# Where split weights begin in memory: token-major units 32 bytes behind a multiple of 128, the others on one

## The chip, the cores and the metric

The kernel runs on one core of one Trainium2 chip. The metric is the device time of one execution in microseconds (us); the median of several runs counts. Before the change three runs took 1570.54, 1565.43 and 1568.50 us.

## The reference, cut to what matters

A decoder trunk of two layers over 256 tokens of width 1024. Each layer is a half-step SwiGLU FFN, a token-mixing sub-layer (a Mamba-2 branch and a gated DeltaNet branch on the same normalised input), and a second half-step FFN. Everything is float32.

```python
for l in range(DEPTH):                                   # DEPTH = 2
    h = h + 0.5 * swiglu(rms_norm(h, ffn1_norm[l]), ffn1_w_in[l], ffn1_w_out[l])
    u = rms_norm(h, mix_norm[l])
    (z_s, xbc, dt_s, qkv, z_d, b_d, a_d, gate_s, gate_d) = jnp.split(u @ w_in[l], split_points, axis=-1)
    y_s = mamba2_branch(z_s, xbc, dt_s, ...)
    y_d = deltanet_branch(qkv, z_d, b_d, a_d, ...)
    merged = (jax.nn.sigmoid(gate_s) * (y_s @ ssm_w_branch[l])
              + jax.nn.sigmoid(gate_d) * (y_d @ dn_w_branch[l]))
    h = h + merged @ w_out[l]
    h = h + 0.5 * swiglu(rms_norm(h, ffn2_norm[l]), ffn2_w_in[l], ffn2_w_out[l])
return rms_norm(h, final_norm)
```

The large products (`u @ w_in`, the FFN's and the projections) hold nearly all of the work.

## The kernel before, in words

**Split weights.** TensorE multiplies in a reduced float32 form (`fp32r`), so each weight is split into a high part and the rest, and a product is made of three: high by high, high by low, low by high. Weights come from memory in forms of 128 rows by 1024 values (4096 bytes in each partition), in an order laid out on the host. `load` brings a form into a raw buffer `wraw` (five of them; a few go into `wfirst`). `prep` makes the two parts of it: ScalarE writes the high part into `whi` (line 66, the helper `act`), VectorE writes the rest into `wlo` (line 69, the helper `tt`). There are five buffers of `whi` and five of `wlo`, used in turn. `take` hands out the next pair of parts and keeps loads and splits some forms ahead.

**Who multiplies with what.** A matmul has a stationary operand of 128x128, loaded by a weight load of its own (PEld in the profile) while an earlier matmul runs, and a moving operand of 256 or 512 columns that streams past it.

- Token-major units (`tok_chunk`, called for `f`, the first four forms of an FFN, and for `t`, the z and gate units of the mixer): the normalised, transposed input `uT` is stationary, the split weights are moving, 512 columns. `mm3`, lines 287 to 289.
- Products with activations made in the kernel (`out_chunks` and `block_products`, results `p`, `o`, `b`): activations `gh`, `gl`, `bsa` to `bsd`, `bh`, `bl`, `mh`, `ml` are stationary, the split weights are moving, 512 columns. Also `mm3`, lines 287 to 289.
- Channel-major units: the split weights are stationary, `uT` is moving. `chan_pair` (`fc`, lines 342 and 346: one matmul of 512 and one of 256 columns) and `chan_chunk` (`kk`, `qq`, `vv`, `xs`, `bc`, `zd`, lines 292 to 294: 256 columns).

The order of the units is written out by hand: `FFN` and `ORDER` at the top of the file, and in them the order of the matmuls on TensorE is fixed.

**Where the buffers lie.** The pools are laid one behind the other in each partition, each tile rounded up to 32 bytes. In the kernel before, by the allocation that its build makes:

| Tiles | First byte | Byte modulo 128 |
|---|---|---|
| `cs` with the identity (`cpool`) | 24704 | 0 |
| `uT` (`cpool`) | 32928 | 32 |
| `wraw`, five of 4096 bytes (`wpool`) | 57984 | 0 |
| `whi`, five of 4096 bytes (`wpool`) | 78464 | 0 |
| `wlo`, five of 4096 bytes (`wpool`) | 98944 | 0 |
| `gh`, `gl`, `bsa`, `bsb`, `bsc`, `mh`, `ml` and all other tiles of `slots` | 119424 and on | 0 |
| `bh`, `bl`, `bsd` and the other 2048-byte tiles of `s2` | 203392 and on | 0 |

The matmuls' operands begin at multiples of 128 bytes within their tiles, so these remainders are those of the operands. The last byte in use is 228128.

Of the kernel before, what the change touches and what calls it, by code (L numbers as in the profile page):

```python
# [8 lines left out]
F32R = mybir.dt.float32r  # L9
I32 = mybir.dt.int32  # L10
AF = mybir.ActivationFunctionType
ALU = mybir.AluOpType
# [4 lines left out]
P = 128  # L17
D = 1024
S = 256
DEPTH = 2  # L20
# [9 lines left out]
NRAW = 5  # L30
NSPL = 5
START = 2

FFN = "f" + 8 * "c" + "A" + 4 * "c" + "A" + 4 * "c" + "A" + 2 * "c" + "A" + 2 * "c" + "BdBBBddddd"
# [7 lines left out]
ORDER = """  # L44
# [7 lines left out]
def trunk_kernel(ctx, tc, x, wst, wsm, norms, lpar, rpar, cst, out):  # L52
    nc = tc.nc
    V, A, G, PE = nc.vector, nc.scalar, nc.gpsimd, nc.tensor

    cpool = ctx.enter_context(tc.tile_pool(name="cpool", bufs=1))
    wpool = ctx.enter_context(tc.tile_pool(name="wpool", bufs=1))
# [7 lines left out]
    def act(o, i, func=AF.Copy, **kw):  # L65
        return A.activation(out=o, in_=i, func=func, **kw)  # L66

    def tt(o, a, b, op):
        return V.tensor_tensor(out=o, in0=a, in1=b, op=op)  # L69
# [9 lines left out]
    def f(ap):  # L79
        return ap.bitcast(F32)  # L80

    def tmp2(name):
        return s2.tile([P, 512], F32, tag="s2", name=name)
# [52 lines left out]
    n_forms = len(plan)  # L136
# [3 lines left out]
    def load(j):  # L140
# [5 lines left out]
        state["last"] = nc.sync.dma_start(r[:], wst[stream[j] // 2, :, (stream[j] % 2) * 1024 :][:, 0:1024])  # L146
        raws[j] = r

    def prep(i):
        kind, js, _ = plan[i]  # L150
        hi = wpool.tile([P, 1024], F32R, tag="whi", name="whi", bufs=NSPL)
        lo = wpool.tile([P, 1024], F32R, tag="wlo", name="wlo", bufs=NSPL)

        def less(o, a, b):
            tt(raws[js[o]][:], raws[js[a]][:], raws[js[b]][:], ALU.subtract)


        r = raws[js[{"q2": 1, "q4": 4, "q5": 3}.get(kind, 0)]]
        with ExitStack() as behind:
            for ins in state["behind"].pop(i, ()):  # L160
                behind.enter_context(tc.issue_after(ins))
            act(hi[:], r[:])
            if kind == "q1":
                less(1, 2, 1)
            elif kind == "q2":
                less(0, 2, 0)
            elif kind == "q4":
                less(0, 3, 0)
            tt(lo[:], r[:], f(hi[:]), ALU.subtract)
            if kind == "q0":  # L170
                less(0, 1, 0)
        for o in {"d": (0,), "q2": (1,), "q3": (2,), "q4": (4,), "q5": (3,), "q6": (0,)}.get(kind, ()):
            raws.pop(js[o])
        halves[i] = (hi, lo)

    def ahead(key, n, fn):
        while state[key] < n:
            fn(state[key])
            state[key] += 1

    def take():
        j = state["taken"]
        state["taken"] = j + 1
        ahead("loaded", min(plan[min(j + NSPL, n_forms) - 1][2] + NRAW - 1, n_raw), load)
        ahead("prepped", min(j + 1 if state["hold"] else j + NSPL, n_forms), prep)
        return halves.pop(j)
# [46 lines left out]
    def rstd_of(t):  # L233

        ss = small([P, 2], "ss")
        for n in range(2):
            junk = tmp2("junk")
            state["square"] = act(junk[:], h[:, t, n * 512 : (n + 1) * 512], AF.Square, scale=1.0 / 32.0, accum_out=ss[:, n : n + 1])
        z = small([P, 2], "zz")
        ts(z[:, 0:1], ss[:, 0:1], ss[:, 1:2], ALU.add, EPS, ALU.add)  # L240
        rsqrt(z[:, 1:2], z[:, 0:1], [P, 1])
        return z[:, 1:2]
# [18 lines left out]
    def norm_in(nw, add=None):  # L261

        for t in range(2):
            with tc.high_priority(offset=PRI), ExitStack() as behind:
                if add:
                    add(t)
                    if t == 0:
                        behind.enter_context(tc.issue_after(state["sums"][5].ins))
                ins, done = rms_chain(t, nw)
            if t == 0:  # L270
                state["hold"] = False
                n = state["taken"]
                if not add:
                    ahead("prepped", n + 1, prep)
                    with tc.issue_after(done[0].ins), tc.issue_after(done[1].ins):
                        ahead("prepped", n + START, prep)
                with tc.issue_after(ins.ins):
                    ahead("prepped", n + 2, prep)
                if add:
                    state["behind"][n + 2] = [d.ins for d in done]  # L280
            elif add:

                state["behind"][n + 4] = (state["square"].ins, ins.ins)
                state["input"] = done
# [946 lines left out]
    for t in range(2):  # L1231
        add(t)
        o = [tmp2("fo") for _ in range(2)]
# [3 lines left out]
        r = rstd_of(t)  # L1237
# [137 lines left out]
```

## Time and profile before

| What | Value |
|---|---|
| Runs | 1570.54, 1565.43, 1568.50 us; median 1568.5 us |
| Profiled execution, first to last instruction (span) | 1565.8 us |
| TensorE (PE) busy | 1545.0 us, 99% of the span, 10152 matmuls |
| Weight loads (PEld) busy | 1342.0 us, 86% |
| VectorE (DVE) busy | 1302.4 us, 83% |
| ScalarE (ACT) busy | 999.8 us, 64% |
| Granted TensorE clock | 0.999 |

The span is the time from the first to the last instruction of the profiled execution; the profile gives no other time for it, and the span lies 2.7 us below the median of the three runs. Matmuls overlap: the duration of one runs from its start to its modelled end, and the next one starts before that end. What a matmul costs is therefore the distance from its start to the start of the next, which the timeline shows; durations can be compared only between matmuls of one shape. In a row `t<-wlo,uT` the tile written stands first, then the moving operand, then the stationary one.

### The profile page before, as it was taken

The numbers are of one execution on the slowest core, as the hardware profiler recorded it, in microseconds if no ns is written. First come the engines' busy times: TensorE is split into PE (matmuls) and PEld (weight loads), VectorE is DVE, ScalarE is ACT, GpSimd is POOL, SyncE is SP. The second block draws the span as 40 slices with busy tenths as digits, with TensorE's granted clock in tenths as the row PEclk, the third lists the DMA queues.
The fourth block names the chain that finished last, engine by engine and source line by source line (L and its number), as shares of the span: only waits on it lengthen the run. The fifth ranks groups of instructions, "written<-read, shape, count | busy, mean of one in ns | idle before, by whom it ended". The sixth has DMA issues, their size and how long they took to land.

```text
span 1565.8 us, 26672 instructions
## 1 busy us (share of the span) xinstructions
PE 1545.0 (99%) x10152; PEld 1342.0 (86%) x10152; DVE 1302.4 (83%) x2048; ACT 999.8 (64%) x1694; POOL 53.2 (3%) x60
## 2 busy tenths in 40 slices
PE   8999999999999999999999999999999999999998
PEld 6888779999888888888788887899998888888886
DVE  6889969957899766899878998699579996679897
ACT  6666668766675655666566676686656666466664
POOL 0000010000000000000000001010000000000000
PEclk9999999999999999999999999999999999999999
DMA  8565565553455555465765566555336546555553
GB/s 298 197 214 188 195 212 173 178 158 118 174 207 173 177 205 196 159 210 177 262 204 187 168 198 223 189 189 189 116 123 213 177 166 212 201 175 166 198 189 134
DMA packets 94215, 292.99 MB, mean 187 GB/s; under 512 B 22325, under 2 KB 23301, under 8 KB 93062
## 3 DMA queue, kind: packets, MB, share of 16 engines
q1 hardware_dynamic: 94086, 291.29, 55.2%
q8 instruction: 79, 1.29, 0.3%
q14 instruction: 50, 0.41, 0.1%
HBM read 289.33 MB, written 1.92 MB: 186 GB/s over the span
## 4 chain that ended last, share of the span: by engine, by line
PE 76%; DVE 13%; DMA 5%; issue 3%; ACT 2%; POOL 1%; SPq 0%; POOLq 0%; DVEq 0%; ACTq 0%
PE fc L342 15%; PE fc L346 8%; DVE wlo L69 7%; PE t L287 3%; PE t L288 3%; PE t L289 3%; DMA wraw<-in_wst_dram 3%; PE b L289 3%; PE b L288 3%; PE b L287 2%; PE xs L292 2%; PE xs L293 2%; PE xs L294 2%; PE o L288 1%; PE o L289 1%
## 5 line engine op out<-in xcount | busy, mean ns | idle before, releaser
L69 DVE TENSOR_TENSOR wlo<-wraw,whi 128x1024 fp32r<-128x1024 f32 x488 | 591.0, 1221 | 139.8 <-ACT whi L66 136.1
L66 ACT ACTIVATE whi<-wraw 128x1024 fp32r<-128x1024 f32 x488 | 511.6, 1057 | 176.4 <-PE b L289 29.8
L342 PE MATMUL fc<-uT,whi 128*128 128x512 f32 x1280 | 445.5, 391 | 0.0
L346 PE MATMUL fc<-uT,wlo 128*128 128x256 f32 x1280 | 360.9, 282 | 0.0
L342 PEld LDWEIGHTS fc<-uT,whi 128*128 128x128 f32 x1280 | 240.3, 188 | 50.7
L346 PEld LDWEIGHTS fc<-uT,wlo 128*128 128x128 f32 x1280 | 241.8, 189 | 0.8
L287 PE MATMUL t<-whi,uT 128*128 128x512 f32 x256 | 102.9, 403 | 0.0
L288 PE MATMUL t<-wlo,uT 128*128 128x512 f32 x256 | 101.5, 396 | 0.2 <-DVE wlo L69 0.2
L289 PE MATMUL t<-whi,uT 128*128 128x512 f32 x256 | 101.5, 397 | 0.0
L66 ACT ACTIVATE whi<-wfirst 128x1024 fp32r<-128x1024 f32 x64 | 67.8, 1059 | 29.7 <-DVE wfirst L69 20.4
L66 ACT ACTIVATE sg<-fc 128x256 f32<-128x256 f32 x80 | 30.6, 382 | 82.3 <-PE fc L346 82.3
L69 DVE TENSOR_TENSOR wlo<-wfirst,whi 128x1024 fp32r<-128x1024 f32 x64 | 78.1, 1220 | 2.0 <-ACT whi L66 1.9
L287 PE MATMUL b<-whi,bh 128*128 128x512 f32 x192 | 76.1, 398 | 0.0
L288 PE MATMUL b<-wlo,bh 128*128 128x512 f32 x192 | 74.9, 390 | 0.0
L289 PE MATMUL b<-whi,bl 128*128 128x512 f32 x192 | 74.3, 394 | 0.3 <-DVE bl L69 0.3
L292 PE MATMUL xs<-uT,whi 128*128 128x256 f32 x256 | 73.1, 286 | 0.0
L294 PE MATMUL xs<-uT,wlo 128*128 128x256 f32 x256 | 71.6, 280 | 0.0
L293 PE MATMUL xs<-uT,whi 128*128 128x256 f32 x256 | 71.4, 279 | 0.0
L288 PE MATMUL o<-wlo,gh 128*128 128x512 f32 x160 | 64.6, 404 | 2.6 <-DVE wlo L69 2.5
L69 DVE TENSOR_TENSOR wfirst<-wraw,wfirst 128x1024 f32<-128x1024 f32 x48 | 58.6, 1220 | 8.9 <-DMA wraw<-in_wst_dram 8.9
L289 PE MATMUL o<-whi,gl 128*128 128x512 f32 x160 | 62.5, 391 | 0.0
L287 PE MATMUL o<-whi,gh 128*128 128x512 f32 x160 | 62.1, 392 | 0.0
(317 smaller groups left out, 3424.5 us busy)
## 6 DMA issues: line engine op xcount, KB each, us to landing
wraw<-in_wst_dram SPq DMA_DIRECT2D x504, 512.0 KB, 4.5
wfirst<-in_wst_dram SPq DMA_DIRECT2D x16, 512.0 KB, 5.8
dc<-rdram SPq DMA_DIRECT2D x8, 1024.0 KB, 8.4
nw<-in_norms_dram SPq DMA_DIRECT2D x6, 512.0 KB, 6.2
gb<-rdram SPq DMA_DIRECT2D x8, 256.0 KB, 5.3
h<-in_x_dram SPq DMA_DIRECT2D x4, 256.0 KB, 5.7
out_dram<-fo SPq DMA_DIRECT2D x4, 256.0 KB, 2.1
dq<-X SPq DMA_DIRECT2D x2, 256.0 KB, 5.0
```

The lines of the kernel that those rows point to most:

```text
L66: return A.activation(out=o, in_=i, func=func, **kw)
L69: return V.tensor_tensor(out=o, in0=a, in1=b, op=op)
L287: PE.matmul(ps, lh, rh, start=start, stop=False)
L288: PE.matmul(ps, lh, rl, start=False, stop=False)
L289: return PE.matmul(ps, ll, rh, start=False, stop=stop)
L292: PE.matmul(ps, wh, mh, start=start, stop=False)
L293: PE.matmul(ps, wh, ml, start=False, stop=False)
L294: PE.matmul(ps, wl, mh, start=False, stop=stop)
L342: PE.matmul(ps[a][:], wh[:, c0 : c0 + P], uT[:, kt].rearrange("p o t -> p (o t)"), start=kt == 0, stop=False,)
L346: PE.matmul(ps[a][:, 0:S], wl[:, c0 : c0 + P], uTh[:, kt, :], start=False, stop=kt == KT - 1)
```

## The change

Each `whi` and `wlo` tile becomes 4192 bytes instead of 4096, and the kernel uses 4096 bytes of it that begin `skip` values into the tile. Because 4192 is 96 more than a multiple of 128, the five buffers of a tag begin at five different remainders; `base` works out the remainder of the buffer that form `i` gets (`turn` is the order in which the buffers are handed out), and `skip` makes up the rest to the place that `places(i)` asks for: 32 bytes behind a multiple of 128 for the forms of the token-major units (`f` and `t` in the list `uses`), a multiple of 128 for every other form. High and low part get the same place. Nothing else is edited; the instructions, their order and their shapes stay.

```diff
+BASE = (0, 96)
...
+    uses = []
+    for _ in range(DEPTH):
+        for sub in range(2):
+            for kind in FFN:
+                uses += {"f": "ffff", "c": "cc", "A": "pppp", "B": "ppp", "d": "o"}[kind]
+            if sub == 0:
+                uses += 4 * "t"
+                for name in ORDER:
+                    uses += {"z": "tt", "g": "tt", "N": 8 * "b"}.get(name[0], "hh" if name[0] in "kqvdbx" and len(name) > 1 else "")
+                uses += 16 * "b" + 8 * "w"
+    assert len(uses) == n_forms, (len(uses), n_forms)
+    turn = [0, 4, 3, 2, 1]
+
+    def places(i):
+        return (1, 1) if uses[i] in "ft" else (0, 0)
+
+    def split_tile(i, o, tag):
+        r = places(i)[o]
+        j = (turn[i % 5], turn[i % 5])[o]
+        base = (BASE[o] + 96 * j) % 128
+        skip = (32 * r - base) % 128 // 4
+        return wpool.tile([P, 1024 + 24], F32R, tag=tag, name=tag, bufs=NSPL)[:, skip : skip + 1024]
+
     def prep(i):
         kind, js, _ = plan[i]
-        hi = wpool.tile([P, 1024], F32R, tag="whi", name="whi", bufs=NSPL)
-        lo = wpool.tile([P, 1024], F32R, tag="wlo", name="wlo", bufs=NSPL)
+        hi = split_tile(i, 0, "whi")
+        lo = split_tile(i, 1, "wlo")
...
-            act(hi[:], r[:])
+            act(hi, r[:])
...
-            tt(lo[:], r[:], f(hi[:]), ALU.subtract)
+            tt(lo, r[:], f(hi), ALU.subtract)
```

## The prediction

> **What bounds the kernel now.** I read the busy times first, then the chain that ended last, the granted clock, and then the stretches in which the touched units run.
>
> ```profile
> span 1565.8 us, 26672 instructions
> PE 1545.0 (99%) x10152; PEld 1342.0 (86%) x10152; DVE 1302.4 (83%) x2048; ACT 999.8 (64%) x1694; POOL 53.2 (3%) x60
> PEclk9999999999999999999999999999999999999999
> PE 76%; DVE 13%; DMA 5%; issue 3%; ACT 2%; POOL 1%; SPq 0%; POOLq 0%; DVEq 0%; ACTq 0%
> 193.10:232.50 39.40, 38.34 (x176) 29.83 (x175) 25.30 (x44) 25.23 (x34) 7.56 (x5) 1.00 0.62 217
> 407.60:423.70 16.10, 15.07 (x75) 12.19 (x74) 13.91 (x16) 9.40 (x15) 1.01 (x1) 1.00 0.44 173
> 439.10:450.00 10.90, 10.90 (x49) 8.80 (x48) 10.30 (x15) 7.80 (x12) 1.60 (x1) 1.00 0.60 193
> 157.70:192.80 35.10, 34.58 (x153) 27.27 (x152) 31.93 (x39) 22.12 (x27) 0.55 (x1) 1.00 0.55 187
> 532.00:579.40 47.40, 47.40 (x227) 39.06 (x226) 29.47 (x39) 25.14 (x37) 0.69 (x1) 1.00 0.64 219
> ```
>
> TensorE is busy in 1545.0 of 1565.8 us at the full clock. The five stretches (length, then busy time of PE, PEld, DVE, ACT, POOL) are three of `t`, one of `o` and one of `b`. PE fills them, or leaves about 1 us; VectorE, the next fullest, is at 10.30 of 10.90 us at its worst. So a nanosecond on a matmul is nearly a nanosecond of the kernel, in either direction. The change adds no instruction and no wait; what it can alter is how long a matmul takes because of where its operands begin. I therefore compare matmuls of one shape (512 columns, stationary 128x128) whose operands begin at different bytes.
>
> ```profile
> L288 PE MATMUL t<-wlo,uT x256: 392/395/501, 193.3 to 1303.0; 128*128 128x512 f32 x128
> L288 PE MATMUL f<-wlo,uT x64: 392/396/794, 10.3 to 1391.3; 128*128 128x512 f32 x64
> L288 PE MATMUL p<-wlo,bsa x48: 389/389/389, 70.8 to 1496.9; 128*128 128x512 f32 x48
> L288 PE MATMUL o<-wlo,gh x160: 387/389/504, 159.3 to 1558.5; 128*128 128x512 f32 x160
> L288 PE MATMUL b<-wlo,bh x192: 387/389/402, 467.8 to 1354.0; 128*128 128x512 f32 x192
> L342 PE MATMUL fc<-uT,whi 128*128 128x512 f32 x1280 | 445.5, 391 | 0.0
> 302.96 0.40 PE L287 MATMUL t<-whi,uT 128*128 128x512 f32 x1
> ...
> 308.56 0.28 PE L292 MATMUL vv<-uT,whi 128*128 128x256 f32 x1
> 96.89 0.39 PE L287 MATMUL p<-whi,gh 128*128 128x512 f32 x1
> ...
> 102.35 0.40 PE L342 MATMUL fc<-uT,whi 128*128 128x512 f32 x1
> ```
>
> The first five rows give smallest, median and largest duration in ns. The same instruction of line 288 takes 389 in `p`, `o` and `b` and 395 to 396 in `t` and `f`. The timeline shows that this is time and not drawing: a `t` unit of 24 matmuls runs from 302.96 to the next unit's start at 308.56, 5.60 us or 233.3 ns each; a `p` block of 24 runs from 96.89 to 102.35, 5.46 us or 227.5 ns each. The price is 5.8 ns by the blocks and 6.5 ns by the medians (395.5 less 389); I take 6.5, since the `p` block opens with matmuls behind a change of unit.
>
> What differs is the place of the stationary operand. In all five the moving weights begin on a multiple of 128 bytes. `bsa`, `gh` and `bh` do too, while `uT` begins 32 bytes behind one. I call stationary remainder minus moving remainder the distance: 0 costs 389; +32 costs 395 to 396. In `fc` the roles are exchanged (`uT` moving, distance -32): mean 391. A weight load runs beside every matmul, so the picture that fits is two streams that read interleaved memory and meet more or less often, depending on their distance.
>
> **The change part by part.**
>
> Gain: the moving weights of `f` and `t` go to 32, where `uT` is, so the distance becomes 0. There are 3 x 256 of `t` and 3 x 64 of `f`, 960 matmuls. At 6.5 ns this is 6.2 us of TensorE. The `t` stretches above leave PE idle for 1.06 of 39.40 and 1.03 of 16.10 us, so a little goes into waits that only begin sooner; I count 85%, 5.3 us. VectorE could become the bound in the stretch at 439.10, which shrinks by 48 x 6.5 = 0.3 us to 10.6, still above its 10.30.
>
> Nothing: the channel-major units. Their stationary weights stay on a multiple of 128 and `uT` stays at 32.
>
> The hidden part: ten buffers grow by 96 bytes, so all that lies behind `wpool` moves by 960 bytes, which is 7 x 128 + 64. If the pools stay packed, every tile of `slots` and `s2` begins at 64 instead of 0: `gh`, `gl`, `bsa` to `bsd`, `bh`, `bl`, `mh`, `ml`. The weights of `p`, `o` and `b` stay at 0. Their distance goes from 0 to +64, which no row of before shows.
>
> ```profile
> L287 PE MATMUL o<-whi,gh x160: 387/389/496, 159.1 to 1558.3; 128*128 128x512 f32 x160
> L287 PE MATMUL o<-whi,mh x64: 387/389/476, 579.6 to 1378.0; 128*128 128x512 f32 x64
> L287 PE MATMUL o<-whi,bsc x16: 389/389/392, 157.7 to 1532.5; 128*128 128x512 f32 x16
> L287 PE MATMUL p<-whi,bsa x48: 389/389/389, 70.6 to 1496.7; 128*128 128x512 f32 x48
> L254 PE MATMUL hnT<-cs,hn 128*128 128x128 f32 x96 | 14.6, 288 | 5.1 <-DVE hn L72 5.1
> L1113 PE MATMUL yT<-cs,yz 128*128 128x128 f32 x64 | 10.2, 272 | 0.0
> L69 DVE TENSOR_TENSOR uT<-hnT,uT 128x512 fp32r<-128x512 f32 x24 | 15.4, 682 | 0.0
> L69 DVE TENSOR_TENSOR ml<-mT,mh 128x512 fp32r<-128x512 f32 x8 | 5.5, 686 | 0.1
> L69 DVE TENSOR_TENSOR wlo<-wraw,whi 128x1024 fp32r<-128x1024 f32 x488 | 591.0, 1221 | 139.8 <-ACT whi L66 136.1
> L66 ACT ACTIVATE whi<-wraw 128x1024 fp32r<-128x1024 f32 x488 | 511.6, 1057 | 176.4 <-PE b L289 29.8
> ```
>
> How many: the row of 160 and that of 64 are one of three each; with `bsb` and `bsd` beside the 16 of `bsc`, `o` has 3 x 256 = 768. `b` has 3 x 192 = 576, and `p` eight each of its sixteen blocks' 24, 384. Together 1728, against 960 that gain. The price of one is bounded below by the smallest duration at distance 0, 387 against 389 (-2 ns), and above by the dearest distance seen, +6.5. Between the ends I take 0: with distances -32 at 391 and 0 at 389 two of three known places are cheap, and the row nearest in kind is these very matmuls at 389. But +64 lies between +32 (dear) and -32 (cheap) on the circle of 128, so the upper end is nearly as likely. The whole is -3.5 to +11.2 us on TensorE, about -3 to +10 at 90%: `b` (47.40 of 47.40 busy) would pay in full, while the `p` blocks are partly covered by VectorE.
>
> Small things: the transposes by the identity (`cs`, stays at 0) read tiles that go to 64; the rows of 96 and 64 stand for the two largest kinds, and at 6.5 ns each such 160 cost 1.0 us; I take 0 and keep +-1. VectorE and ScalarE: a subtraction that reads and writes `uT` at 32 takes 682 ns, the same shape into `ml` at 0 takes 686, so the place of an operand costs them nothing that I can see; a difference of 4 ns on 488 subtractions would be 2 us of an engine with 17% to spare, hidden under TensorE. The raw buffers lie ahead of the moved tiles, so the loads and SP's queue keep times and addresses.
>
> The sum: -5.3 + 0 + 0 gives 1565.8 - 5.3 = 1560.5 us for the span, and against the median, which lies 2.7 us above the profiled span, 1568.5 - 5.3 = 1563.2 us.
>
> Here a rule speaks against any effect. The Trainium skill, "TensorE: Matmul & The Clock Gate", section "Part 2: What happens when you issue a matmul", says that matmul stream and weight load have read ports of their own: "Loading the next tile's weights doesn't steal SBUF read bandwidth from the running matmul." By it the sum would be 0 and the time 1568.5. The trace does not sit well with it: 389 against 395 for one shape at one clock wants a cause that the rule does not offer.
>
> **The rivals.**
>
> *The products pay (slower).* At distance +64 the 1728 matmuls of `p`, `o`, `b` cost 6.5 ns more each. 11.2 us at 90% is 10.1; with the gain, 1568.5 - 5.3 + 10.1 = 1573.3. It takes the gain away from 5.3 / (1728 x 0.9) = 3.4 ns on. For it: the position between +32 and -32, and that two moving operands at 0 are all it needs. Against: nothing in the rows, they only don't show it.
>
> *The load's own alignment decides (slower).* If a stationary operand away from a multiple of 128 is what costs, whatever the moving one does, `t` and `f` stay at 395 and `p`, `o`, `b` go up to it: 1568.5 + 10.1 = 1578.6. For it: all dear rows have the stationary operand at 32, all cheap ones at 0, `fc` included.
>
> *Nothing moves.* The place modulo 128 is not the cause (`uT` lies elsewhere in memory than `gh`, and the streams do not meet): 1568.5. Against: `bh`, `gh` and `bsa` lie far apart in memory and all have 389. This is what the rule of the Trainium skill cited above, in "TensorE: Matmul & The Clock Gate", would give.
>
> *Half prices.* Distance +64 at 3.4 ns: gain and loss cancel, 1568.5.
>
> *All gain.* Distance +64 at -2 ns: -5.3 - 3.1, 1560.1.
>
> **How the numbers follow.** About 0.3%, 4.7 us, is what a measurement of this kernel can tell from no change. The forecast has 0.42; being only 5.3, I count 0.31 of it as faster and 0.11 as same. Products pay 0.22 (+4.8 at the full price, more where distance +64 is dearer still: 0.20 slower, 0.02 same). The load's own alignment 0.14, slower. Nothing moves 0.11, half prices 0.05, both same. All gain 0.06, of which 0.05 faster, 0.01 same. Faster 0.36, same 0.30, slower 0.34. The range runs from 1560.0, all gain, to 1579.0, the load's own alignment; the forecast alone would have 1561.5 to 1565.0.
>
> **What would show it.** Right: the median of `t<-wlo,uT` and `f` falls from 395 to 389 and a `t` unit of 24 takes 5.44 us; `p`, `o`, `b` stay at 389, a `p` block at 5.46; `fc` stays at 391; VectorE's subtraction stays at 1221. The first rival shows as `t` at 389 with `p`, `o`, `b` at 395 or above, the second as `t` at 395 and `p`, `o`, `b` there too. It is wrong if those medians do not move at all, or if `t` rises. If the medians move as forecast and the span does not, the saved time has gone into idle time of PE behind `wlo`.

## The result, and the profile after

The changed kernel takes 1573.61 us (median of six runs, 1572.19 to 1576.3) against 1567.44 us for the kernel before (six runs): ratio 1.0036, 95% interval 1.0023 to 1.0049. It is slower by 6.2 us by these medians and by 5.6 us by the ratio, where 5.3 us less was forecast.

The page of the changed kernel, its first two lines and the chain:

```profile
span 1574.5 us, 26672 instructions
PE 1552.4 (99%) x10152; PEld 1342.8 (85%) x10152; DVE 1303.5 (83%) x2048; ACT 1001.7 (64%) x1694; POOL 53.1 (3%) x60
PE 76%; DVE 12%; DMA 6%; issue 3%; ACT 2%; POOL 1%; SPq 0%; POOLq 0%; DVEq 0%; ACTq 0%
```

TensorE is busy 7.4 us longer (1552.4 against 1545.0) with the same 10152 matmuls; VectorE and ScalarE are within 2 us of before, and the chain's shares within one point. So the place to look is the time of a matmul. The same groups by tile as in the prediction (smallest, median, largest duration in ns), then the page's row of `fc`, then the same `p` block of 24 matmuls on the timeline:

```profile
L312 PE MATMUL t<-wlo,uT x256: 387/393/500, 194.5 to 1308.3; 128*128 128x512 f32 x128
L312 PE MATMUL f<-wlo,uT x64: 387/393/796, 10.7 to 1397.3; 128*128 128x512 f32 x64
L312 PE MATMUL p<-wlo,bsa x48: 388/392/398, 71.5 to 1503.6; 128*128 128x512 f32 x48
L311 PE MATMUL p<-whi,bsa x48: 388/394/398, 71.2 to 1503.4; 128*128 128x512 f32 x48
L312 PE MATMUL o<-wlo,gh x160: 388/393/505, 160.6 to 1567.1; 128*128 128x512 f32 x160
L312 PE MATMUL b<-wlo,bh x192: 388/392/403, 469.2 to 1359.8; 128*128 128x512 f32 x192
```

```profile
L366 PE MATMUL fc<-uT,whi 128*128 128x512 f32 x1280 | 447.5, 393 | 0.0
```

```profile
97.71 0.40 PE L311 MATMUL p<-whi,gh 128*128 128x512 f32 x1
...
103.26 0.40 PE L366 MATMUL fc<-uT,whi 128*128 128x512 f32 x1
```

`t` and `f` fell from 395 and 396 to 393, not to 389. `p`, `o` and `b` rose from 389 to 392 to 394, and what was 389 in every one of 48 now runs from 388 to 398. `fc`, which was to stay, rose from 391 to 393. The `p` block takes 5.55 us (103.26 less 97.71), 231.3 ns a matmul against 227.5.

Summed from start to start over the whole of each trace, `p`, `o` and `b` take 6.3 us more, `t` and `f` 2.3 us less, `fc` 2.0 more, the mixer's channel-major units 2.4 more; with 0.2 us of the rest this is 8.6 of the 8.7 us between the two spans. The profiled execution of the changed kernel is the longest of its six (1576.3 us), so these sums are somewhat larger than the difference of the medians.

### The profile page after: what moved, and what is told of

Its sections match the earlier page's. It is cut to its first block, busy times and chain, and to the rows that moved or that the text cites. A ratio compares the mean times of both kernels' runs of the same rounds, so it can differ in the third digit from the quotient of the medians.

```text
span 1574.5 us, 26672 instructions
## 1 busy us (share of the span) xinstructions
PE 1552.4 (99%) x10152; PEld 1342.8 (85%) x10152; DVE 1303.5 (83%) x2048; ACT 1001.7 (64%) x1694; POOL 53.1 (3%) x60
## 4 chain that ended last, share of the span: by engine, by line
PE 76%; DVE 12%; DMA 6%; issue 3%; ACT 2%; POOL 1%; SPq 0%; POOLq 0%; DVEq 0%; ACTq 0%
PE fc L366 16%; PE fc L370 8%; DVE wlo L70 6%; DMA wraw<-in_wst_dram 3%; PE t L312 3%; PE t L311 3%; PE t L313 3%; PE b L313 3%; PE b L311 3%; PE b L312 3%; PE p L313 2%; PE p L311 2%; PE p L312 2%; PE o L313 1%; PE o L312 1%
## 5 line engine op out<-in xcount | busy, mean ns | idle before, releaser
L70 DVE TENSOR_TENSOR wlo<-wraw,whi 128x1024 fp32r<-128x1024 f32 x488 | 590.8, 1221 | 143.7 <-ACT whi L67 141.3
L67 ACT ACTIVATE whi<-wraw 128x1024 fp32r<-128x1024 f32 x488 | 513.3, 1058 | 186.1 <-PE b L313 28.4
L67 ACT ACTIVATE whi<-wfirst 128x1024 fp32r<-128x1024 f32 x64 | 67.7, 1058 | 30.4 <-DVE wfirst L70 20.0
L70 DVE TENSOR_TENSOR wlo<-wfirst,whi 128x1024 fp32r<-128x1024 f32 x64 | 78.0, 1219 | 2.1 <-ACT whi L67 1.9
```

## The experiments

Two readings were tested. Theory A is the first rival of the prediction: only the remainder modulo 128 matters, and the tiles moved by 64 bytes are what costs. Theory B came from the trace after: there the matmuls fall into groups if the distance (stationary start less moving start) is taken modulo 256. `p`, `o` and `b` take 232.3 ns from start to start at 64 and 230.4 at 192; `t` and `f` take 229.3 at 0 and 232.0 at 128. Modulo 128 the change's five buffers begin at four remainders, not five (0, 96, 64, 32, 0), and `skip` evens these out; modulo 256 it does not. By the allocation of the changed kernel's build the forms stand at one of two places 128 bytes apart: the place changes at four of five steps from one form to the next, and in about one form of five the high and the low part differ by 128 too. So high and low part get the same place modulo 128 only, and the distance jumps by 128 again and again.

In what follows a time "from start to start" is the mean over a group's matmuls, without those that waited (over 245 ns for 512 columns, over 130 for 256); by this measure before has 227.8 for `p`, `o`, `b`, 233.1 for `t` and `f`, 346.9 for a pair of `fc` and 116.8 for the other channel-major units. Groups that an experiment does not touch repeat within 0.5 ns (`p`, `o`, `b` at distance 0: 227.8 to 228.2 in six traces). Ratios are to the kernel before on the same chip, with the 95% interval behind them.

**The moved tiles alone** (e1_pad64):

```diff
+    gap = ctx.enter_context(tc.tile_pool(name="gap", bufs=1))
+    gap.tile([P, 16], F32, name="gap")
     slots = ctx.enter_context(tc.tile_pool(name="slots", bufs=1))
```

> The kernel before with 64 unused bytes behind wpool, so that the stationary tiles of p, o and b lie 64 further and all else stays. Theory A (the remainder modulo 128 decides, and the change was slower because of these moved tiles alone): p, o and b rise from 227 to the 231 ns from start to start that they have after the change, 1728 x 4 = 7 us, ratio 1.004. Theory B (the distance counts modulo 256, and distances that differ from one form to the next cost too): all of p, o, b now have the one distance 64, for which the trace after shows 232.3, so 1728 x 5.6 = 9.7 us, ratio 1.006. In both t stays at 395 (median duration of t<-wlo,uT, ns) and fc at 391.

Measured: 1.0027 (1.0018 to 1.0036). `p`, `o`, `b` 233.2 from start to start, the rest as before. The rows by tile of this kernel, and `fc` in the kernel before (last):

```profile
L290 PE MATMUL o<-wlo,gh x160: 392/394/504, 160.8 to 1567.2; 128*128 128x512 f32 x160
L290 PE MATMUL t<-wlo,uT x256: 392/395/501, 194.7 to 1308.2; 128*128 128x512 f32 x128
L344 PE MATMUL fc<-uT,whi x1280: 390/390/481, 25.4 to 1531.6; 128*128 128x512 f32 x183
L342 PE MATMUL fc<-uT,whi x1280: 390/390/484, 24.4 to 1524.7; 128*128 128x512 f32 x183
```

The mechanism of the first rival is real, 5.4 ns a matmul: a distance of +64 is dear. By the ratio the kernel is 4.2 us slower, less than either theory forecast (1.004 and 1.006), though a matmul at 233.2 is above both forecasts (231 and 232.3). In the one profiled execution the `p`, `o` and `b` matmuls take 7.6 us more; it is a long one among its twelve (1576.34 us, median 1574.3).

**The moved tiles back, in the changed kernel** (e2_after_pad64): the same two lines added to the changed kernel.

> The changed kernel with 64 unused bytes more behind wpool, so that the moved tiles are back on a multiple of 256 bytes. Theory A: p, o and b are back at 389 median duration and 227 from start to start, t keeps what it gained; 1573.6 - 7 = 1566.6, ratio to before 0.9995 or less. Theory B: the split buffers stand on multiples of 128, every other one of them off a multiple of 256, so p, o and b have distances 0 and 128 by turns, about 230 ns; 1573.6 - 1728 x 1.3 = 1571.4, ratio 1.0025; fc stays at 348 ns for its pair of matmuls, against 346.7 before.

Measured: 1.0034 (1.0020 to 1.0048), no different from the change's 1.0036. `p`, `o`, `b` go from 231.4 to 230.9 only, `t` and `f` stay at 230.7, `fc`'s pair at 348.4. This is where theory A falls: with every moved tile back on its old remainder, the loss is still there. Theory B's ratio of 1.0025 lies within the interval.

**128 bytes, which modulo 128 is nothing** (e3_pad128): as e1_pad64 with `gap.tile([P, 32], ...)`.

> The kernel before with 128 unused bytes behind wpool. Theory A: nothing changes, p, o, b at 389, ratio 1.000. Theory B: one distance of 128 everywhere in p, o, b, for which the trace after shows 231.7 in t: 1728 x 5 = 8.6 us, ratio 1.005, median duration 393 to 395.

Measured: 1.0024 (1.0013 to 1.0034). `p`, `o`, `b` at 232.5, everything else as before:

```profile
L290 PE MATMUL o<-wlo,gh x160: 390/393/505, 160.4 to 1563.6; 128*128 128x512 f32 x160
L290 PE MATMUL t<-wlo,uT x256: 392/396/501, 194.2 to 1305.9; 128*128 128x512 f32 x128
```

So the distance does not count modulo 128. Theory B's 8.6 us was too much: 3.8 us were measured.

**The step of 4192 alone** (e5_after_t0): e2_after_pad64 with the place of `f` and `t` undone.

```diff
-        return (1, 1) if uses[i] in "ft" else (0, 0)
+        return (0, 0)
```

> The changed kernel with the 64 unused bytes of e2_after_pad64, and with the forms of f and t put on a multiple of 128 like all others, so that only the buffers' step of 4192 bytes is left of the change. Theory A (remainder modulo 128): every remainder is that of before, t 233, p, o, b 227, ratio 1.000. Theory B (distance modulo 256, and it settles only where it stays the same for several matmuls): high and low part and successive forms differ by 128, so p, o, b stay near 230.5 and fc's pair at 348 as in e2_after_pad64; t has 32 and 160 by turns, 231 to 234; 3 us or less above e2_after_pad64's 1576.3, ratio 1.0035 to 1.0055.

Measured: 1.0044 (1.0031 to 1.0056). Modulo 128 this kernel has every operand where the kernel before has it. `p`, `o`, `b` are at 231.0, `fc`'s pair at 348.4, the other channel-major units at 117.6, `t` and `f` at 233.4. The buffers' step is what the change costs; the place of `f` and `t` takes back about 1 part in 1000 of the time (1.0044 to 1.0034, measured on two chips with intervals that overlap; 233.4 to 230.7 in the traces).

**`uT` moved instead of the weights** (e4_uT0):

```diff
+    cpool.tile([P, 56], F32, name="ahead_of_uT")
     uT = cpool.tile([P, KT, 2, S], F32R, name="uT")
+    cpool.tile([P, 8], F32, name="behind_uT")
```

> The kernel before with 224 unused bytes ahead of uT and 32 behind it, so that uT alone moves against all other tiles and stands on the same remainder of 256 as the split weights; buffers stay 4096 bytes apart. Both theories: t and f go to 389 and 226.7 from start to start, 960 x 6.5 x 0.85 = 5.3 us less. For fc and the other channel-major units the distance goes from -32 to 0, which neither theory has a row for: fc's pair of 346.7 ns somewhere from 340 (two matmuls as cheap as in p) to 351, so the time from 1553 to 1568; ratio 0.9965 if they stay.

Measured: 1.0057 (1.0040 to 1.0073), 1578.85 us, above the forecast range of 1553 to 1568. The group rows of its profile, then two by tile, then `xs` in the kernel before:

```profile
L344 PE MATMUL fc<-uT,whi 128*128 128x512 f32 x1280 | 451.9, 397 | 0.0
L348 PE MATMUL fc<-uT,wlo 128*128 128x256 f32 x1280 | 359.3, 281 | 0.0
```

```profile
L290 PE MATMUL t<-wlo,uT x256: 387/389/500, 196.0 to 1311.1; 128*128 128x512 f32 x128
L295 PE MATMUL xs<-uT,whi x256: 278/283/287, 384.7 to 1285.5; 128*128 128x256 f32 x128
L293 PE MATMUL xs<-uT,whi x256: 277/279/282, 380.3 to 1276.9; 128*128 128x256 f32 x128
```

The forecast's own step comes true: `t` at 389, 227.8 from start to start, where its distance is 0 modulo 256 and stays so. But the channel-major units, with `uT` moving, lose more than that at distance 0: 352.0 for `fc`'s pair against 346.9, 119.9 for the others against 116.8.

**One remainder of 256 for all buffers, `f` and `t` shifted** (e6_even), shown against the kernel before, cut to the places; `uses` is the list of the change, and `wsc` moves to make room:

```diff
+    def places(i):
+        return {"f": 32, "t": 32, "c": 0, "h": 0}.get(uses[i], 0)
+
+    def split_tile(i, o, tag):
+        skip = places(i) // 4
+        return wpool.tile([P, 1024 + 64], F32R, tag=tag, name=tag, bufs=NSPL)[:, skip : skip + 1024]
...
-        wsc = cpool.tile([P, KT, 2, 48], F32R, tag="wsc", name="wsc")
+        wsc = slots.tile([P, KT, 2, 48], F32R, tag="y3", name="wsc")
```

> Buffers of 4352 bytes (17 x 256), so that all ten stand on one remainder of 256; the forms of f and t begin 32 bytes into them, where uT is, all others at their start. Room for it comes from wsc, moved from cpool into a free tile of slots (3072 bytes, 12 x 256). Nothing else moves against 256. Theory B: t and f settle at 226.7 as in e4_uT0, fc stays at 346.7 for its pair, xs at 116.7, p, o, b at 226.7; 960 x 6.5 x 0.85 = 5.3 us less than before, ratio 0.9965. Theory A: the same 5.3 us. A third reading, that any mixing of distances between units costs: less gain, ratio 0.998 to 1.000.

Measured: 0.9985 (0.9976 to 0.9994), faster than before. Its page, and rows by tile:

```profile
PE 1541.3 (98%) x10152; PEld 1341.0 (86%) x10152; DVE 1302.1 (83%) x2048; ACT 998.6 (64%) x1694; POOL 53.2 (3%) x60
```

```profile
L309 PE MATMUL t<-wlo,uT x256: 387/389/504, 193.8 to 1301.6; 128*128 128x512 f32 x128
L309 PE MATMUL o<-wlo,gh x160: 387/389/507, 159.6 to 1558.1; 128*128 128x512 f32 x160
L363 PE MATMUL fc<-uT,whi x1280: 390/390/484, 24.7 to 1523.1; 128*128 128x512 f32 x183
```

All prices are those that the forecast wanted (`t` and `f`, `p`, `o` and `b` 227.9, `fc`'s pair 346.9, the others 116.8). The gain is 2.4 us, not 5.3. The number is inside the 0.998 to 1.000 of the third reading, that any mixing of distances between units costs, but no group of matmuls has become dearer, so its mechanism does not show. What shows is waiting. Between the two profiled executions the matmuls that waited (over the limits above) take 3.8 us more: 1.7 in `o`, 1.1 in `xs`, 0.7 in `t`, 0.4 in `f`. In `o` the weight loads wait 13.1 us for VectorE's low parts instead of 10.5, of which 2.9 and 2.5 us show as idle time of the matmuls. These are single executions, and the runs of one kernel differ by more than this; that the waits are what is missing was not tested.

This run also settles the period. Its buffers stand 4352 = 17 x 256 bytes apart, so modulo 512 the distances of `p`, `o`, `b` still change between 0 and 256. Sorted by that, they take 228.0 and 227.8 ns: 256 bytes is a shift that costs nothing.

**The table of prices** (e7_c64, e8_c96, e9_c128, e10_c160, e11_c192): e6_even with other numbers in `places`, one profile each.

```diff
-        return {"f": 32, "t": 32, "c": 0, "h": 0}.get(uses[i], 0)
+        return {"f": 32, "t": 32, "c": 64, "h": 64}.get(uses[i], 0)      # e7_c64
+        return {"f": 32, "t": 32, "c": 96, "h": 96}.get(uses[i], 0)      # e8_c96
+        return {"f": 32, "t": 32, "c": 128, "h": 128}.get(uses[i], 32)   # e9_c128
+        return {"f": 32, "t": 32, "c": 160, "h": 160}.get(uses[i], 96)   # e10_c160
+        return {"f": 32, "t": 32, "c": 192, "h": 192}.get(uses[i], 64)   # e11_c192
```

> As e6_even, with the forms of the channel-major units 64 bytes into their buffers, 32 behind uT's remainder. One price of the table is looked for: fc's pair (346.7 at -32, 352.1 at 0) and xs (116.7 and 120.0). Theory B, if the price is a smooth function of the distance: dearer than at 0 or like it, 352 and 120, 10 us slower. Theory A makes no other number.

> As e7_c64, with 96 bytes, a distance of +64 for the channel-major units. If the price is a smooth function of the distance: between that of 0 and that of 96 (fc's pair 346.4 in stretches of the changed kernel, xs 118.0), so 347 to 352 and 118 to 120, 0 to 8 us slower than e6_even.

> As e6_even, with the channel-major forms 128 bytes into their buffers (distance +96) and those of p, o and b 32 bytes (distance -32). Theory B takes its prices from stretches of the changed kernel with one distance: fc's pair 346.4 ns, xs 118.0 and so 0 to 2 us slower than e6_even for these units; for p, o, b the circle has -32 between -64 (230.4) and 0 (226.7), 228 to 231, 2 to 7 us slower. If the price counted modulo 128, +96 would be the -32 of before: 346.7 and 116.7.

> Distance +128 for the channel-major units, -96 for p, o and b. Modulo 128 the first would be the 0 of e4_uT0 (fc's pair 352.1, xs 120.0), the second the +32 of t before (233.3). Theory B has no row for either; if prices change smoothly over the circle of 256, fc's pair lies near 346 to 349 and p, o, b at 230 to 233.

> Distance +160 (-96) for the channel-major units, -64 for p, o and b. Modulo 128 the first would be the +32 of e7_c64 (fc's pair 352.7, xs 118.3). Theory B: fc's pair between 346 and 350; p, o, b at 230.4, as stretches of the changed kernel have it at 192, or below it where it settles, 228 to 230.4, 3 to 6 us slower than e6_even.

The single executions took 1579.53, 1572.05, 1576.58, 1579.74 and 1581.25 us, in this order (before on the same chip: median 1570.73 us for the first two, one run of 1571.7 for the others). Single runs have no interval, so what counts here is the price of a matmul. Measured, in ns from start to start, each distance being the same for all matmuls of the kind in its kernel:

| Distance modulo 256 | 0 | 32 | 64 | 96 | 128 | 160 | 192 | 224 |
|---|---|---|---|---|---|---|---|---|
| weights moving, 512 columns (`t`, `f`, `p`, `o`, `b`) | 227.9 | 233.1 | 233.2 | - | 232.5 | 233.5 | 229.5 | 233.2 |
| `fc`, pair of 512 and 256, weights stationary | 352.0 | 352.6 | 353.1 | 346.7 | 350.9 | 350.1 | - | 346.9 |
| other channel-major units, 256 columns | 119.9 | 118.3 | 115.8 | 118.1 | 119.0 | 119.9 | - | 116.8 |

The prices are no smooth function: for moving weights all of +32, +64, +128, +160 and -32 are dear and -64 is nearly cheap; for `fc` +96 is as good as -32, for the other units +64 is the best. Of theory B's forecasts, `fc` held in e7_c64, both channel-major kinds in e9_c128, and `p`, `o`, `b` in e11_c192; the other units of e7_c64, both kinds of e8_c96, `p`, `o`, `b` of e9_c128 and `fc` of e10_c160 missed, and `p`, `o`, `b` of e10_c160 (233.5 against 230 to 233) and `fc` of e11_c192 (350.1 against 346 to 350) fell just outside. Theory B is thus right about the period and does not foretell the prices.

**The best place of each kind** (e12_best): `places` with 32 for `f` and `t`, 96 for the mixer's channel-major units (`h`), 0 for the rest.

> The best place seen for each kind, in the buffers of e6_even: f and t 32 bytes in (distance 0), the FFN's fc at the start (distance -32, pair 346.9), the mixer's channel-major units 96 bytes in (distance +64, 115.8 ns against 116.8), p, o and b at the start (distance 0). Theory B: e6_even's gain and 2688 x 1.0 = 2.7 us x 0.85 = 2.3 us more, ratio 0.997. If half of a gain on TensorE is lost again to waits, as e6_even lost it, ratio 0.9978.

Measured: 0.9966 (0.9953 to 0.9979), 1565.15 us against 1570.19. It beats both kernels, by as much as was forecast (0.997). By tile, `kk` has 276 (first) where before has 278 (second) to 280:

```profile
L314 PE MATMUL kk<-uT,whi x128: 276/276/282, 234.5 to 1035.3; 128*128 128x256 f32 x128
L293 PE MATMUL kk<-uT,whi x128: 277/278/281, 234.0 to 1036.5; 128*128 128x256 f32 x128
```

**What steps of 128 cost beyond their mean price.** The table gives most of the change's price by itself. In the changed kernel's trace 875 of the counted `p`, `o`, `b` matmuls stand at 64 and 776 at 192; their mean by the table is 231.5, and 231.4 was measured. `t` and `f` stand at 0 and 128 about equally, 230.2 by the table and 230.6 measured; the other channel-major units at 96 and 224, 117.5 and 117.6. `fc` is the exception: 96 and 224 cost 346.7 and 346.9 a pair where each stays, and 348.5 where they alternate, so its 2.0 us are the price of changing the distance. A pair whose high and low part differ takes 350.9, the others 347.5 and 348.3 in the mean.

A settling time goes with this. In the changed kernel a `t` unit has six matmuls on one form before the next form comes, and distances 0 and 128. For matmuls of `t` whose distance was 0, was 0 in the next one too and had been 0 for one, two, ... six matmuls before, the times from start to start are, in the mean:

| matmuls at distance 0 before it | 1 | 2 | 3 | 4 | 5 | 6 |
|---|---|---|---|---|---|---|
| ns | 231.7 | 230.3 | 228.2 | 227.5 | 227.5 | 226.7 |
| count | 48 | 46 | 44 | 41 | 16 | 7 |

In the kernel before, `o` does the same behind an interruption (232.6, 233.2, 230.6, 228.9 for the first four, 226.9 from the ninth on) and then keeps it. The price of distance 0 is thus a state that takes from three to nine matmuls to reach. For `t` and `f` it adds to the mean price no more than the 0.4 ns above.

## Why the prediction was wrong

**What bounds the kernel: right.** TensorE stayed at 99%, no wait took its place, and the time moved with the matmuls.

**The step that failed: distances were counted modulo 128.** All three terms of the sum rest on it. It was -5.3 for `t` and `f`, 0 for `p`, `o`, `b` and 0 for the channel-major units; the traces show -2.3, +6.3 and +4.4 us.

**The gain of `t` and `f`: right in kind, mis-sized.** Distance 0 is worth the 5 to 6 ns (233.1 to 227.8 in e4_uT0, 389 in the row), but the change does not give distance 0. It gives 0 or 128 modulo 256 by turns. I had taken over the 128 of the change's own arithmetic without asking whether rows of before show that period; in before all ten buffers had one remainder of 256 as well, so they could not. Term in the sum: -6.2 us on TensorE, measured -2.3.

**"Nothing: the channel-major units": wrong.** Their remainders modulo 128 did stay, and they cost 4.4 us more (2.0 for `fc`, 2.4 for the others), for the same reason: about half of them stand at 96 instead of 224, which is dearer for the others (118.1 against 116.8) and costs `fc` by the changes alone. e5_after_t0 shows it with nothing left but the step.

**The price of `p`, `o`, `b`: the value 0, taken from two cheap neighbours, was wrong.** It measured +3.6 ns on 1728 matmuls, inside the bounds of -2 and +6.5. But the move by 64 bytes, the reason given for the upper bound, is not needed for it: with the tiles moved back it is +3.1. The step puts these matmuls at 64 and 192 with the move and at 0 and 128 without it, and by the table the two mixes cost nearly the same (231.5 and 230.3).

**The first rival had the time, 1573.3 against 1573.6 measured, and not the cause.** Its mechanism exists (e1_pad64, 1.0027) and adds next to nothing in the changed kernel (1.0036 with it, 1.0034 without). That its number was met is luck: a smaller gain, a smaller price and a cost that it did not name happen to add up to it.

**The second rival, the load's own alignment, is out.** In e6_even `t` has both operands 160 behind a multiple of 256 and takes 227.9; in e4_uT0 both are at 128 and it takes 227.8. In e9_c128 the weights of `p`, `o`, `b` stand where those of `t` stand, with another distance, and cost 233.2. The distance decides. "Nothing moves" is out by e1_pad64.

**The rule of ports.** The Trainium skill, "TensorE: Matmul & The Clock Gate", section "Part 2: What happens when you issue a matmul", says that loading the next weights takes no read bandwidth from the running matmul. The measurement decides here: moving the stationary tiles alone by 64 or 128 bytes makes the same matmuls 5.4 and 4.7 ns longer, though no run shows that it is bandwidth that they lose. The Trainium skill's page "SBUF — State Buffer", section "Operand start alignment", says of its own measurements that they are about legality, not speed, and timed nothing; these runs time it.

**The small things held.** VectorE's subtraction took 1221 ns before and after, ScalarE's copy 1057 and 1058, the raw loads 4.5 us to landing in both.

What stays open: why the prices stand in this order. A meeting of two read streams fits that only their distance counts and that a stretch has to settle, but no run looks at the streams themselves.

## What to carry to other kernels

Where TensorE is full, compare the time of equal matmuls between units before anything else: 6 ns on 395 is visible in the medians by tile, and it is worth moving a tile for. A rule of placement read off a kernel whose buffers all share one remainder says nothing about its own period; test it with a shift that the rule calls nothing, as the 128 bytes did here. And when tiles are padded, work out what the padding does to every operand behind them and to the step from one buffer to the next.

## What the runs showed of the hardware

- The mean time from start to start of matmuls with 512 columns and moving weights goes from 227.9 to 233.5 ns with the distance of the starts of stationary and moving operand, modulo 256 bytes: a uniform shift by 128 bytes costs 4.7 ns, distances 256 apart took 228.0 and 227.8. Which absolute address both have makes no difference that shows (227.8 and 227.9).
- Which distance is good is not one rule for all units: 0 for 512 columns with the weights moving, 96 and 224 for `fc`'s pair of 512 and 256 with the weights stationary, 64 for the other units of 256 columns. Whether columns, roles or the alternation of shapes decides was not separated.
- After a change of distance it took three to six matmuls until the time at distance 0 settled (from 231.7 to 226.7 ns), after an interruption some nine.
- VectorE, ScalarE and the loads show none of this: 1219 to 1221 ns for the two kinds of subtraction that write `wlo`, 1057 and 1058 ns for the copy into `whi`, 4.5 us for a load into `wraw`, before and after.
